# A decoder trunk: whole normalized inputs made beside three biased tiles, later tiles multiplied side by side

## The chip, the cores and the metric

One Trainium2 chip (trn2), one core. The metric is the device time of one execution in microseconds (us); the median of the runs shown is compared. The engines are TensorE (PE; its weight loads are PEld), VectorE (DVE), ScalarE (ACT), GpSimd (POOL) and SyncE (SP, which issues the loads).

## What is computed

```
x = x + 0.5 * gate * swiglu(modulate(x), w_in, w_out)      # FFN 1 (layer 0), FFN 3 (layer 1)
x = x + gate * mixer(modulate(x))                          # retention (layer 0), short_conv (layer 1)
x = x + 0.5 * gate * swiglu(modulate(x), w_in, w_out)      # FFN 2 (layer 0), FFN 4 (layer 1)
out = rmsnorm(x, final_g)

def modulate(x, g, shift, scale): return rmsnorm(x, g) * (1 + scale) + shift
def swiglu(h, w_in, w_out):       gate, up = h @ w_in (halves);  return (silu(gate) * up) @ w_out
def short_conv(h, ...):           b, c, u = h @ w_in (thirds);   return (b * conv_w3(c * u)) @ w_out
```

Two layers, 256 tokens, width 1024, FFN width 2816. Shift, scale and gate come from `silu(c) @ ada_w + ada_b`, a vector times 75 MB of weights.

## The kernel before, in words

Activations lie transposed: eight tiles `x[k]` of 128 features by 256 tokens. All products have float32 accuracy: a weight block w and an input h are each split into a high part `hi`, rounded to float32r, and a low part `lo`, the exact rest, and w h is summed as hi_w hi_h + hi_w lo_h + lo_w hi_h (`product`, line 273). Where the two input halves lie side by side and the PSUM row is wide enough (line 282), the first two are one 512-column matmul whose halves are added later; else there are three matmuls.

Weights stream through five raw buffers. `prepare` (line 250) splits a tile of 2048 columns in two pieces of 1024: ACT casts `hi` (line 243), DVE or, for one piece in six, POOL subtracts `lo` (line 248). There are six `hi` and six `lo` buffers, three tiles' worth; `AHEAD` keeps four tiles in the program's order of loading. Between them `run_side` and `reduce_loaded` run the ada work: one DVE reduction of 128x1024 per half of an ada tile (line 119), paced by `pace`.

An FFN makes 22 projection tiles, each of two sums over eight blocks (`projections`, line 289), then the output products; the convolution makes 12 projection tiles. The RMS norm's factor r (one number per token) isn't known when the projections start, so they run on h = x * scale, and `normalized` (line 302) multiplies the sums by r in one DVE operation. The shift enters through two extra columns (`S1 = S + 2`): line 390 puts the shift's split into columns 256 and 257 of h, a matmul has 258 columns, and the projection's own bias comes out in column 256, to be added by the later activation (`bias=y[:, 0, S:S + 1]`, lines 553 to 556, 725 to 728 and 746 to 748). `modulated` (line 411) issues tile 1 of a sublayer block by block (`by_part`), then the sum of squares over features (line 338), the root on ACT (line 350) and its reciprocal r on DVE (line 356). `retention` works on the same h and is not changed.

The order of the instructions on each engine isn't written by hand but laid out by the Tile scheduler from the program's order and its priorities; an engine runs its own list strictly in that order. PSUM has four pairs of banks (`banks`, line 79); one holds a copy of `cond` from the 11th tile of FFN 1 on (line 567).

Of the kernel before, what the change touches and what calls it, by code (L numbers as in the profile page):

```python
# [14 lines left out]
P = 128  # L15
D = 1024
S = 256
# [11 lines left out]
DEPTH = 2  # L29
PRIO = 300  # L30
LATE = 5
AHEAD = 4
FILL = 8
PARTS = (((0, 2, 0, 0), (5, 8, 1, 1), (2, 5, 0, 0)), ((0, 3, 0, 1), (6, 8, 1, 0), (3, 6, 0, 1)))
# [31 lines left out]
def trunk_kernel(ctx: ExitStack, tc: tile.TileContext, a: dict, out: bass.AP):  # L66
# [4 lines left out]
    wraw_p = ctx.enter_context(tc.tile_pool(name="wraw", bufs=5))  # L71
    whi_p = ctx.enter_context(tc.tile_pool(name="whi", bufs=6))
    wlo_p = ctx.enter_context(tc.tile_pool(name="wlo", bufs=6))
    slot_p = ctx.enter_context(tc.tile_pool(name="slot", bufs=22))
    xhl_p = ctx.enter_context(tc.tile_pool(name="xhl", bufs=1))
    tmp = ctx.enter_context(tc.tile_pool(name="tmp", bufs=2))
    psum = ctx.enter_context(tc.tile_pool(name="psum", bufs=4, space=bass.MemoryType.PSUM))
# [6 lines left out]


    misc = const.tile([P, C_END], F32, name="misc")
    cond = const.tile([P, D], F32, name="cond")
    table = const.tile([P, T_END], F32, name="table")
    ones = const.tile([P, P], F32, name="ones")
    eps = const.tile([P, 1], F32, name="eps")  # L90
# [144 lines left out]
    def split_high(raw, width, w, step=SPLIT):  # L235

        c = w["done"]
        m = min(step, width - c)
        if c % SPLIT == 0:
            hi, lo = whi_p.tile([P, SPLIT], F32R, name="hi"), wlo_p.tile([P, SPLIT], F32R, name="lo")  # L240
            w["parts"].append((hi, lo))
        hi, lo = (part[:, c % SPLIT:c % SPLIT + m] for part in w["parts"][-1])
        nc.scalar.copy(out=hi, in_=raw[:, c:c + m])  # L243
        w["done"] += m
        return lo, raw[:, c:c + m], hi.bitcast(F32)
# [40 lines left out]
                nc.tensor.matmul(out=ps, lhsT=hi, rhs=m[:, 1], start=False, stop=False)  # L286
            nc.tensor.matmul(out=ps[:, :n], lhsT=lo, rhs=m[:, 0], start=False, stop=stop)  # L287

    def projections(h, by_part=False):

        ps, w = banks(), weights()
        n = h[0].shape[-1]
        if by_part:
            for k in range(KB):
                for i in range(2):
                    product(ps[:, i, :n], w, i * KB + k, [h[k]], k == 0, k == KB - 1)
        else:
            for i in range(2):
                product(ps[:, i, :n], w, i * KB, h, True, True)
        return ps  # L300

    def normalized(ps, r, n=S1):

# [101 lines left out]
    def fill(n):  # L405

        ps = banks()[:, 1, :P]
        for _ in range(n):
            nc.tensor.matmul(out=ps, lhsT=ones, rhs=cond[:, :P], start=True, stop=True)

    def modulated():

        h = norm.pop("h")
        state["after"] = norm.pop("made")
        ps = projections(h, True)
        std = rms([norm.pop("acc")], D)  # L420
        with behind():
            load_table(AF.Silu, std)
            return h, inverse(std), std, ps

    def first_modulated():

        l, s = sublayers[0]
        parts = []
        engines = {mybir.EngineType.Activation, mybir.EngineType.DVE, mybir.EngineType.Pool}
        with tc.manual_schedule(engines=engines):  # L430
            for i, pair in enumerate(x_pairs):
                nc.sync.dma_start(out=pair, in_=a["x"][:, 2 * i:2 * i + 2, :])
# [12 lines left out]
            for k in range(KB):  # L445
                ada_reduce(l, s, k, ada.pop(), True)
                if k % 2 == 0:
                    pair = tmp.tile([P, 2, S], F32, name=f"xs{k}", bufs=1)
                xs = pair[:, k % 2, :]
                nc.scalar.activation(out=xs, in_=x[k], func=AF.Copy, scale=scale_t[l][s][:, k:k + 1])  # L450
                raw, width, w = load(2)
                if k + 1 < KB:
                    ada.append(ada_load(l, s, k + 1, 2))
                first = split_high(raw, width, w, 512)
                h = xhl_p.tile([P, 2, HALF], F32R, name=f"h{k}")[:, :, :S]
                parts.append(halves(l, s, k, xs, std, h))
                plain.append((xs, raw))
                split_low(*first, nc.vector)
                for c in range(1, WHOLE // 512):
                    split_low(*split_high(raw, width, w, 512), nc.vector)  # L460
                if k == 1:
                    load_table(AF.Silu, std)
            r = inverse(std)
        state["after"] = [i.ins for i in parts[-1][1:]]
        return [p[0] for p in parts], r
# [72 lines left out]
                    nc.tensor.matmul(out=out, lhsT=lo, rhs=h[k][:, 0], start=False, stop=stop)  # L538
        return [ps.rearrange("p (n s) -> p n s", s=S) for ps in pss]

    def ffn(n, h, r, begun=None):
        act = []

        def activate(ps):
            n = h[0].shape[-1]
            y = normalized(ps, r, n)
            sg = tmp.tile([P, S], F32, name="sg")
            av = tmp.tile([P, S], F32, name="av", bufs=3)
            if n == S:
                nc.scalar.activation(out=sg, in_=y[:, 0, :S], func=AF.Silu)  # L550
                nc.vector.tensor_tensor(out=av, in0=sg, in1=y[:, 1, :S], op=ALU.mult)
            else:
                nc.scalar.activation(out=sg, in_=y[:, 0, :S], func=AF.Silu, bias=y[:, 0, S:S + 1])  # L553
                nc.vector.scalar_tensor_tensor(  # L554
                    out=av, in0=y[:, 1, :S], scalar=y[:, 1, S:S + 1], in1=sg, op0=ALU.add, op1=ALU.mult
                )
            t = in_halves(slot(F32R, "act"))
            split(t, av, nc.gpsimd)
            act.append(t)

        for ps in first_projections(h) if n == 0 else [begun]:
            activate(ps)
        while len(act) < FB:
            activate(projections(h))
            if n == 0 and len(act) == KEEP:
                kept = banks().rearrange("p n c -> p (n c)")
                nc.scalar.copy(out=kept, in_=cond)
                state["cond"] = kept
# [147 lines left out]
        for d in range(2, KB):  # L716
            output(n, d, [(weights(), 0, gated)])

    def short_conv(n, h, r, begun):
        gated = []  # L720

        def taps(d, y, cv):
            u = tmp.tile([P, S], F32, name="u", tag="sg")
            z = tmp.tile([P, S], F32, name="z", tag="av", bufs=3)
            nc.scalar.activation(out=u, in_=y[:, 1, :S], func=AF.Identity, bias=y[:, 1, S:S + 1])
            nc.vector.scalar_tensor_tensor(
                out=z, in0=y[:, 0, :S], scalar=y[:, 0, S:S + 1], in1=u, op0=ALU.add, op1=ALU.mult
            )
            tap = [misc[:, C_CONV + i * KB + d:C_CONV + i * KB + d + 1] for i in range(3)]
            nc.scalar.activation(out=cv, in_=z, func=AF.Copy, scale=tap[2])  # L730
            for i, sh in ((1, 1), (0, 2)):
                nc.vector.scalar_tensor_tensor(
                    out=cv[:, sh:], in0=z[:, :S - sh], scalar=tap[i], in1=cv[:, sh:], op0=ALU.mult, op1=ALU.add
                )

        convs = []
        for d in range(KB):
            if d % 2 == 0:
                pair = slot(F32, "conv")
            convs.append(pair[:, d % 2 * S:(d % 2 + 1) * S])  # L740
            taps(d, normalized(projections(h) if d else begun, r), convs[d])
        for d2 in range(KB // 2):
            y = normalized(projections(h), r)
            for i in range(2):
                yc = y[:, i, :S]
                nc.vector.scalar_tensor_tensor(
                    out=yc, in0=yc, scalar=y[:, i, S:S + 1], in1=convs[2 * d2 + i], op0=ALU.add, op1=ALU.mult
                )
                t = in_halves(slot(F32R, "yg"))
                split(t, yc, nc.gpsimd if d2 < KB // 2 - 1 else nc.vector)  # L750
                gated.append(t)
# [8 lines left out]

    for n, (l, s) in enumerate(sublayers):
        if n == 0:
            ffn(n, *first_modulated())
            continue
        h, r, std, begun = modulated()
        if s != 1:
            ffn(n, h, r, begun)
        elif l % 2 == 0:
            retention(n, h, r, std, begun)
        else:  # L770
            short_conv(n, h, r, begun)
# [87 lines left out]
```

## Time and profile before

| | us |
|---|---|
| runs shown (3) | 1109.13, 1111.17, 1112.13; median 1111.17 |
| profiled execution, its own time | 1109.17 |
| its span | 1107.4 |
| PE busy | 1073.8 |
| DVE, ACT, POOL busy | 850.2, 575.4, 387.7 |
| FFN 2's projections and output stage | 427.9 to 556.5, 556.5 to 618.8 |
| FFN 3's projections and output stage | 618.8 to 747.0, 747.0 to 809.3 |
| convolution's projections | 809.3 to 879.8 |
| FFN 4's projections | 903.3 to 1034.4 |

The profile shows one execution. Busy time counts an engine's instructions; the chain of waits follows the work that ended last back to what released it. A row of instructions gives start, duration, engine, line, operation, output <- inputs. Matmuls are pipelined, so their durations overlap: what a stretch of matmuls costs is read from the start of its first to the start of what follows.

### The profile page before, as it was taken

How to read it: one execution, taken by the hardware profiler on the slowest of the kernel's cores; microseconds unless marked ns; L12 is line 12 of the kernel's file. 1: busy time of each engine (PE TensorE's matmuls, PEld its weight loads, DVE VectorE, ACT ScalarE, POOL GpSimd, SP SyncE). 2: the span in 40 equal slices, each digit the busy share in tenths (PEclk: the TensorE clock that was granted, in tenths of full speed). 3: DMA queues.
4: the chain of work that ended last, by engine and by line, in shares of the span. 5: the costliest groups of instructions: out<-in, count | busy, mean ns of one | idle time of the engine just before them, and what ended most of it. 6: DMA issues, size and time to landing. Idle time of an engine off the chain costs nothing.

```text
span 1107.4 us, 19630 instructions
## 1 busy us (share of the span) xinstructions
PE 1073.8 (97%) x7790; PEld 1019.1 (92%) x7790; DVE 850.2 (77%) x1118; ACT 575.4 (52%) x918; POOL 387.7 (35%) x345
## 2 busy tenths in 40 slices
PE   8999999997899999999999999999999989999996
PEld 7999988996779989999988999998899989999985
DVE  5999777999559888887768778776798786666354
ACT  4464454732357666455455655445565475454452
POOL 0034356344024631333355232335511532223352
PEclk9999999998999999999999999999999999999998
DMA  9977789855465777786669867667886535454441
GB/s 348 354 272 277 295 283 316 308 205 190 190 228 191 265 249 278 289 312 247 244 225 321 326 251 301 253 229 252 313 300 253 175 138 207 167 191 132 157 131 39
DMA packets 44574, 268.52 MB, mean 242 GB/s; under 512 B 4801, under 2 KB 6977, under 8 KB 19906
## 3 DMA queue, kind: packets, MB, share of 16 engines
q1 hardware_dynamic: 43138, 266.56, 66.4%
q8 instruction: 61, 1.00, 0.4%
q10 hardware_dynamic: 1344, 0.71, 0.2%
q14 instruction: 31, 0.25, 0.1%
HBM read 266.20 MB, written 1.05 MB: 241 GB/s over the span
## 4 chain that ended last, share of the span: by engine, by line
PE 58%; DVE 2%; issue 0%; ACT 0%; DVEq 0%; ACTq 0%
PE ps L287 19%; PE ps L286 14%; PE ps L285 14%; PE ps L283 10%; DVE lo L248 1%; PE ps L338 0%; DVE rsum L475 0%; DVE h L392 0%; DVE raw L781 0%; DVE r L777 0%; DVE x L478 0%; ACT hi L243 0%; DVEq L854 0%; DVE x L480 0%; ACT std L350 0%
## 5 line engine op out<-in xcount | busy, mean ns | idle before, releaser
L248 DVE TENSOR_TENSOR lo<-raw,hi 128x1024 fp32r<-128x1024 f32 (+1 forms) x300 | 363.1, 1218 | 174.8 <-ACT hi L243 144.6
L285 PE MATMUL ps<-h,hi 128*128 128x258 f32 (+1 forms) x1728 | 490.2, 284 | 3.6 <-DVE sum L610 2.5
L286 PE MATMUL ps<-h,hi 128*128 128x258 f32 (+1 forms) x1728 | 489.9, 283 | 1.6 <-DVE h L392 1.5
L287 PE MATMUL ps<-h,lo 128*128 128x258 f32 (+1 forms) x1728 | 490.3, 284 | 0.0
L243 ACT CAST hi<-raw 128x1024 fp32r<-128x1024 f32 (+2 forms) x408 | 377.3, 937 | 205.8 <-PE ps L286 104.5
L285 PEld LDWEIGHTS ps<-h,hi 128*128 128x128 f32 x1728 | 329.4, 191 | 4.5 <-issue 3.2
L286 PEld LDWEIGHTS ps<-h,hi 128*128 128x128 f32 x1728 | 329.0, 190 | 2.6 <-DVE h L392 1.3
L287 PEld LDWEIGHTS ps<-h,lo 128*128 128x128 f32 x1728 | 329.0, 190 | 0.0
L248 POOL TENSOR_TENSOR lo<-raw,hi 128x384 fp32r<-128x384 f32 (+1 forms) x108 | 203.2, 1882 | 311.4 <-ACT hi L243 302.0
L283 PE MATMUL ps<-act,hi 128*128 128x512 f32 x616 | 216.0, 395 | 0.6 <-DVE rsum L475 0.6
L287 PE MATMUL ps<-act,lo 128*128 128x256 f32 x704 | 197.4, 280 | 0.0
L312 POOL TENSOR_TENSOR act<-av,act 128x256 fp32r<-128x256 f32 x88 | 84.4, 961 | 250.6 <-ACT act L311 241.5
L119 DVE CUSTOM_DVE_ANT_0 raw<-raw,ps,misc 128x1024 f32<-128x1024 f32 x124 | 154.4, 1273 | 0.0
L283 PEld LDWEIGHTS ps<-act,hi 128*128 128x128 f32 x616 | 115.4, 187 | 28.1 <-DVE rsum L475 1.7
L287 PEld LDWEIGHTS ps<-act,lo 128*128 128x128 f32 x704 | 133.1, 189 | 0.3 <-DVE lo L248 0.3
L311 ACT CAST act<-av 128x256 fp32r<-128x256 f32 x88 | 35.5, 405 | 100.8 <-DVE av L554 78.6
L305 DVE TENSOR_TENSOR sum<-ps,r 128x516 f32<-128x516 f32 (+1 forms) x108 | 73.9, 688 | 16.1 <-PE ps L287 15.8
L554 DVE SCALAR_TENSOR_TENSOR av<-sum,sg 128x256 f32<-128x256 f32 x66 | 51.8, 784 | 17.6 <-ACT sg L553 17.6
L553 ACT ACTIVATE sg<-sum 128x256 f32<-128x256 f32 x66 | 33.5, 508 | 25.7 <-DVE sum L305 25.5
L321 ACT ACTIVATE sq<-x 128x256 f32<-128x256 f32 x48 | 19.8, 416 | 49.5 <-DVE x L478 42.3
L328 POOL TENSOR_TENSOR acc<-acc,sq 128x256 f32<-128x256 f32 x32 | 27.1, 846 | 36.9 <-ACT sq L321 34.4
L283 PE MATMUL ps<-og,hi 128*128 128x512 f32 x112 | 38.9, 391 | 0.0
(126 smaller groups left out, 1079.2 us busy)
## 6 DMA issues: line engine op xcount, KB each, us to landing
raw<-in_ffn_in SPq DMA_DIRECT2D x80, 1024.0 KB, 4.9
raw<-in_ada_w SPq DMA_DIRECT2D x64, 1024.0 KB, 5.7
raw<-in_ffn_out SPq DMA_DIRECT2D x64, 704.0 KB, 5.0
raw<-in_ada_w SPq DMA_DIRECT2D x16, 512.0 KB, 6.1
raw<-in_ffn_in SPq DMA_DIRECT2D x16, 512.0 KB, 7.0
raw<-in_ret_qk SPq DMA_DIRECT2D x8, 1024.0 KB, 6.4
raw<-in_ret_v SPq DMA_DIRECT2D x8, 1024.0 KB, 4.9
raw<-in_ret_g SPq DMA_DIRECT2D x8, 1024.0 KB, 4.8
```

Of the source, the lines that this page charges most:

```text
L119: ins = nc.vector.tensor_tensor_reduce(out=w, in0=w, in1=state["cond"], scale=1.0, scalar=misc[:, C_ADAB + 72 * l + col:C_ADAB + 72 * l + ...
L243: nc.scalar.copy(out=hi, in_=raw[:, c:c + m])
L248: eng.tensor_tensor(out=lo, in0=raw, in1=hi, op=ALU.subtract)
L283: nc.tensor.matmul(out=ps, lhsT=hi, rhs=m.rearrange("p n s -> p (n s)"), start=start, stop=False)
L285: nc.tensor.matmul(out=ps, lhsT=hi, rhs=m[:, 0], start=start, stop=False)
L286: nc.tensor.matmul(out=ps, lhsT=hi, rhs=m[:, 1], start=False, stop=False)
L287: nc.tensor.matmul(out=ps[:, :n], lhsT=lo, rhs=m[:, 0], start=False, stop=stop)
L305: nc.vector.tensor_tensor(out=y[:, :, :n], in0=ps[:, :, :n], in1=r[:, :n].unsqueeze(1).to_broadcast([P, 2, n]), op=ALU.mult)
L311: hi = nc.scalar.copy(out=dst[:, 0], in_=src)
L312: lo = eng.tensor_tensor(out=dst[:, 1], in0=src, in1=dst[:, 0].bitcast(F32), op=ALU.subtract)
L553: nc.scalar.activation(out=sg, in_=y[:, 0, :S], func=AF.Silu, bias=y[:, 0, S:S + 1])
L554: nc.vector.scalar_tensor_tensor(out=av, in0=y[:, 1, :S], scalar=y[:, 1, S:S + 1], in1=sg, op0=ALU.add, op1=ALU.mult)
```

## The change

In FFNs 2 to 4 and the convolution the first three projection tiles stay as they were (`BIASED = 3`). Beside them a new function `whole` makes the complete normalized input, x * r * scale + shift, split in halves that lie side by side in eight slots, and the remaining tiles multiply these: 512 columns for the high weights, 256 for the low, no bias columns, no r behind them. The two halves of each sum are added by an ACT copy of the second and a DVE addition of the first. The fourth tile is issued block by block. The slot pool grows from 22 to 30, `cond` moves from a constant to one of the six `hi` buffers (and to PSUM later, as before), and four pairs `xs` of FFN 1 move into slots.

```diff
+BIASED = 3
...
-    slot_p = ctx.enter_context(tc.tile_pool(name="slot", bufs=22))
+    slot_p = ctx.enter_context(tc.tile_pool(name="slot", bufs=30))
...
-    cond = const.tile([P, D], F32, name="cond")
+    cond = whi_p.tile([P, D], F32, name="cond", tag="hi")
...
-    def projections(h, by_part=False):
+    def projections(h, by_part=False, side=False):
...
-        n = h[0].shape[-1]
+        n = h[0].shape[-1] * (2 if side else 1)
...
+    def projected(src):
+
+        src["used"] += 1
+        if src["used"] <= BIASED:
+            y = normalized(src.pop("begun") if src["used"] == 1 else projections(src["h"]), src["r"])
+            return y, [y[:, i, S:S1] for i in range(2)]
+        ps = projections(src["whole"], src["used"] == BIASED + 1, True)
+        y = tmp.tile([P, 2, HALF], F32, name="sum")
+        nc.scalar.copy(out=y[:, :, :S], in_=ps[:, :, S:])
+        nc.vector.tensor_tensor(out=y[:, :, :S], in0=ps[:, :, :S], in1=y[:, :, :S], op=ALU.add)
+        return y, None
...
+    def whole(n, r):
+
+        l, s = sublayers[n]
+        parts = []
+        for k in range(KB):
+            xr = tmp.tile([P, S], F32, name="xr", tag="sq", bufs=3)
+            (nc.gpsimd if k % 2 else nc.vector).tensor_tensor(out=xr, in0=x[k], in1=r[:, :S], op=ALU.mult)
+            nc.scalar.activation(
+                out=xr, in_=xr, func=AF.Identity, scale=scale_t[l][s][:, k:k + 1],
+                bias=mod[l][:, 24 * s + k:24 * s + k + 1],
+            )
+            h = in_halves(slot(F32R, "whole"))
+            split(h, xr, nc.vector)
+            parts.append(h)
+        return parts
...
-                    pair = tmp.tile([P, 2, S], F32, name=f"xs{k}", bufs=1)
+                    pair = in_halves(slot(F32, "xs"))
...
-    def ffn(n, h, r, begun=None):
+    def ffn(n, src=None, h=None, r=None):
...
-        for ps in first_projections(h) if n == 0 else [begun]:
-            activate(ps)
+        if n == 0:
+            for ps in first_projections(h):
+                activate(normalized(ps, r, S), None)
+        else:
+            src["whole"] = whole(n, src["r"])
         while len(act) < FB:
-            activate(projections(h))
+            if n:
+                activate(*projected(src))
+            else:
+                activate(normalized(projections(h), r, S), None)
...
-    def short_conv(n, h, r, begun):
+    def short_conv(n, src):
         gated = []
+        src["whole"] = whole(n, src["r"])
...
-            taps(d, normalized(projections(h) if d else begun, r), convs[d])
+            taps(*projected(src), convs[d])
         for d2 in range(KB // 2):
-            y = normalized(projections(h), r)
+            y, _ = projected(src)
```

In `activate` and `taps` a tile without bias uses plain products where a biased one adds the bias in the same operation, and `taps` then needs no `u`.

How the order moves, at the start of FFN 3. First DVE's list, from the reciprocal on. Before (`lo` is a weight subtraction, `sum` the evacuation of a projection tile, `av` the product of gate and up):

```order
L356 RECIPROCAL r<-std 128x256
L248 TENSOR_TENSOR lo<-raw,hi 128x1024
L305 TENSOR_TENSOR sum<-ps,r 128x2x258
L248 TENSOR_TENSOR lo<-raw,hi 128x1024
L554 SCALAR_TENSOR_TENSOR av<-sum,sg 128x256
L305 TENSOR_TENSOR sum<-ps,r 128x2x258
L248 TENSOR_TENSOR lo<-raw,hi 128x1024
```

And with the change (`xr` is x times r, `whole` the low half of a part; of the eight `xr` four are here, the others on POOL):

```order
L375 RECIPROCAL r<-std 128x256
L249 TENSOR_TENSOR lo<-raw,hi 128x1024
L436 TENSOR_TENSOR xr<-x_91,r 128x256
L436 TENSOR_TENSOR xr<-x_92,r 128x256
L324 TENSOR_TENSOR sum<-ps,r 128x2x258
L249 TENSOR_TENSOR lo<-raw,hi 128x1024
L331 TENSOR_TENSOR whole<-xr,whole 128x256 x3
L436 TENSOR_TENSOR xr<-x_93,r 128x256
L586 SCALAR_TENSOR_TENSOR av<-sum,sg 128x256
L324 TENSOR_TENSOR sum<-ps,r 128x2x258
L249 TENSOR_TENSOR lo<-raw,hi 128x1024
L331 TENSOR_TENSOR whole<-xr,whole 128x256 x2
```

The parts' steps stand between evacuations and weight subtractions, which keep their sequence; after the rows shown come one more `xr`, an `av`, a `whole`, the evacuation of tile 3, a `lo` and the last two `whole`.

Then ACT's list at the same place with the change, from the second of two weight casts behind the root on (`sg` is the silu of a biased tile):

```order
L244 CAST hi<-raw 128x1024 x2
L437 ACTIVATE xr<-xr,mod_96,sc_100 128x256 x3
L330 CAST whole<-xr 128x256 x3
L319 ACTIVATE sg<-sum 128x256
L244 CAST hi<-raw 128x1024
L437 ACTIVATE xr<-xr,mod_96,sc_100 128x256 x2
L330 CAST whole<-xr 128x256 x2
L437 ACTIVATE xr<-xr,mod_96,sc_100 128x256
```

Before, the casts and the silu stood there alone; the first activation of a part now stands behind a cast that waits for a `hi` buffer.

## Rows read from the trace of the kernel before

**Rows 1.** The page: busy time, share of the span, instructions of each engine.

```profile
PE 1073.8 (97%) x7790; PEld 1019.1 (92%) x7790; DVE 850.2 (77%) x1118; ACT 575.4 (52%) x918; POOL 387.7 (35%) x345
```

**Rows 2.** The page: chain that ended last, share of the span by engine, by line.

```profile
PE 58%; DVE 2%; issue 0%; ACT 0%; DVEq 0%; ACTq 0%
PE ps L287 19%; PE ps L286 14%; PE ps L285 14%; PE ps L283 10%; DVE lo L248 1%; PE ps L338 0%; DVE rsum L475 0%; DVE h L392 0%; DVE raw L781 0%; DVE r L777 0%; DVE x L478 0%; ACT hi L243 0%; DVEq L854 0%; DVE x L480 0%; ACT std L350 0%
```

**Rows 3.** PE in projection stretches: start:end length, busy (instructions), granted clock, DMA share, GB/s.

```profile
434.80:556.51 121.71, 121.71 (x1010) 1.00 0.73 268
618.79:624.55 5.76, 5.76 (x51) 1.00 1.03 393
624.79:747.05 122.26, 122.26 (x1010) 1.00 0.71 260
815.36:879.77 64.41, 64.41 (x530) 1.00 0.65 231
912.16:1034.43 122.27, 122.27 (x1011) 1.00 0.50 171
```

**Rows 4.** The same in output stages of FFN 2 and the convolution.

```profile
579.59:610.33 30.74, 30.74 (x176) 1.00 0.91 322
880.12:898.84 18.72, 18.72 (x110) 1.00 0.41 154
```

**Rows 5.** Groups by form: count, busy us, mean ns; idle us before, its releasers.

```profile
L248 DVE TENSOR_TENSOR lo<-raw,hi 128x1024 fp32r<-128x1024 f32 x276 | 348.0, 1264 | 174.8 <-ACT hi L243 144.6 <-PE ps L287 29.4
...
L119 DVE CUSTOM_DVE_ANT_0 raw<-raw,ps,misc 128x1024 f32<-128x1024 f32 x124 | 154.4, 1273 | 0.0
...
L305 DVE TENSOR_TENSOR sum<-ps,r 128x512 f32<-128x512 f32 x22 | 14.6, 681 | 0.2
...
L672 ACT COPY o<-ps 128x512 f32<-128x512 f32 x8 | 4.5, 584 | 0.0
...
L725 ACT ACTIVATE u<-sum 128x256 f32<-128x256 f32 x8 | 4.1, 509 | 6.1 <-DVE sum L305 6.1
...
L312 DVE TENSOR_TENSOR hv<-xs,hv 128x256 fp32r<-128x256 f32 x8 | 3.3, 413 | 0.1
L311 ACT CAST hv<-xs 128x256 fp32r<-128x256 f32 x8 | 3.2, 406 | 30.2 <-DVE xs L402 30.2
```

**Rows 6.** Waits, first 145 us: engine line <- waited for: us, times, longest.

```profile
ACT act L311 <- DVE av L551: 20.9, 12, 2.8
```

**Rows 7.** Instructions of POOL from 447 to 638: start, us, what.

```profile
447.83 2.40 POOL L248 TENSOR_TENSOR lo<-raw,hi 128x1024 fp32r<-128x1024 f32 x1 [1.91 <-ACT hi L243]
...
635.20 1.47 POOL L312 TENSOR_TENSOR act<-av,act 128x256 fp32r<-128x256 f32 x1 [6.09 <-ACT act L311]
637.48 0.74 POOL L312 TENSOR_TENSOR act<-av,act 128x256 fp32r<-128x256 f32 x1 [0.80 <-ACT act L311]
```

**Rows 8.** Instructions of DVE in the same stretch.

```profile
447.92 3.39 DVE L248 TENSOR_TENSOR lo<-raw,hi 128x1024 fp32r<-128x1024 f32 x1
451.24 0.47 DVE L554 SCALAR_TENSOR_TENSOR av<-sum,sg 128x256 f32<-128x256 f32 x1
...
636.00 0.96 DVE L554 SCALAR_TENSOR_TENSOR av<-sum,sg 128x256 f32<-128x256 f32 x1
```

**Rows 9.** DVE at the start of FFN 3.

```profile
628.88 1.75 DVE L356 RECIPROCAL r<-std 128x256 f32<-128x256 f32 x1
630.55 1.16 DVE L248 TENSOR_TENSOR lo<-raw,hi 128x1024 fp32r<-128x1024 f32 x1
```

**Rows 10.** ACT at the start of FFN 3.

```profile
630.86 1.06 ACT L243 CAST hi<-raw 128x1024 fp32r<-128x1024 f32 x1 [1.79 <-PE ps L286]
```

**Rows 11.** DVE at the starts of FFN 2, the convolution and FFN 4.

```profile
436.50 1.75 DVE L356 RECIPROCAL r<-std 128x256 f32<-128x256 f32 x1
...
817.72 1.74 DVE L356 RECIPROCAL r<-std 128x256 f32<-128x256 f32 x1
...
913.06 1.75 DVE L356 RECIPROCAL r<-std 128x256 f32<-128x256 f32 x1
```

More of the change, by code (lines that the diff above doesn't have):

```diff
@@ L239, in split_high @@
         if c % SPLIT == 0:
-            hi, lo = whi_p.tile([P, SPLIT], F32R, name="hi"), wlo_p.tile([P, SPLIT], F32R, name="lo")
+            hi, lo = whi_p.tile([P, SPLIT], F32R, name="hi", tag="hi"), wlo_p.tile([P, SPLIT], F32R, name="lo")
             w["parts"].append((hi, lo))
@@ L300, in projections, with silu @@
         return ps
+    def projected(src):
[8 more added lines that the diff above has]
+        return y, None
+    def silu(y, i, bias, out):
+        if bias is None:
+            nc.scalar.activation(out=out, in_=y[:, i, :S], func=AF.Silu)
+        else:
+            nc.scalar.activation(out=out, in_=y[:, i, :S], func=AF.Silu, bias=bias[i][:, :1])
     def normalized(ps, r, n=S1):
@@ L539, in first_projections, with activate @@
         return [ps.rearrange("p (n s) -> p n s", s=S) for ps in pss]
-    def ffn(n, h, r, begun=None):
+    def ffn(n, src=None, h=None, r=None):
         act = []
-        def activate(ps):
-            n = h[0].shape[-1]
-            y = normalized(ps, r, n)
+        def activate(y, bias):
             sg = tmp.tile([P, S], F32, name="sg")
             av = tmp.tile([P, S], F32, name="av", bufs=3)
-            if n == S:
-                nc.scalar.activation(out=sg, in_=y[:, 0, :S], func=AF.Silu)
+            silu(y, 0, bias, sg)
+            if bias is None:
                 nc.vector.tensor_tensor(out=av, in0=sg, in1=y[:, 1, :S], op=ALU.mult)
             else:
-                nc.scalar.activation(out=sg, in_=y[:, 0, :S], func=AF.Silu, bias=y[:, 0, S:S + 1])
                 nc.vector.scalar_tensor_tensor(
-                    out=av, in0=y[:, 1, :S], scalar=y[:, 1, S:S + 1], in1=sg, op0=ALU.add, op1=ALU.mult
+                    out=av, in0=y[:, 1, :S], scalar=bias[1][:, :1], in1=sg, op0=ALU.add, op1=ALU.mult
                 )
@@ L559, in activate @@
             act.append(t)
-        for ps in first_projections(h) if n == 0 else [begun]:
-            activate(ps)
+        if n == 0:
[3 more added lines that the diff above has]
+            src["whole"] = whole(n, src["r"])
         while len(act) < FB:
-            activate(projections(h))
+            if n:
+                activate(*projected(src))
+            else:
+                activate(normalized(projections(h), r, S), None)
             if n == 0 and len(act) == KEEP:
@@ L717, in retention, with taps @@
             output(n, d, [(weights(), 0, gated)])
-    def short_conv(n, h, r, begun):
+    def short_conv(n, src):
         gated = []
-        def taps(d, y, cv):
-            u = tmp.tile([P, S], F32, name="u", tag="sg")
+        src["whole"] = whole(n, src["r"])
+        def taps(y, bias, cv):
             z = tmp.tile([P, S], F32, name="z", tag="av", bufs=3)
[L725 to L728, printed above, removed]
+            if bias is None:
+                nc.vector.tensor_tensor(out=z, in0=y[:, 0, :S], in1=y[:, 1, :S], op=ALU.mult)
+            else:
+                u = tmp.tile([P, S], F32, name="u", tag="sg")
+                nc.scalar.activation(out=u, in_=y[:, 1, :S], func=AF.Identity, bias=bias[1][:, :1])
+                nc.vector.scalar_tensor_tensor(
+                    out=z, in0=y[:, 0, :S], scalar=bias[0][:, :1], in1=u, op0=ALU.add, op1=ALU.mult
+                )
             tap = [misc[:, C_CONV + i * KB + d:C_CONV + i * KB + d + 1] for i in range(3)]
@@ L740, in short_conv @@
             convs.append(pair[:, d % 2 * S:(d % 2 + 1) * S])
-            taps(d, normalized(projections(h) if d else begun, r), convs[d])
+            taps(*projected(src), convs[d])
         for d2 in range(KB // 2):
-            y = normalized(projections(h), r)
+            y, _ = projected(src)
             for i in range(2):
                 yc = y[:, i, :S]
-                nc.vector.scalar_tensor_tensor(
-                    out=yc, in0=yc, scalar=y[:, i, S:S + 1], in1=convs[2 * d2 + i], op0=ALU.add, op1=ALU.mult
-                )
+                nc.vector.tensor_tensor(out=yc, in0=yc, in1=convs[2 * d2 + i], op=ALU.mult)
                 t = in_halves(slot(F32R, "yg"))
@@ L762, in trunk_kernel @@
         if n == 0:
-            ffn(n, *first_modulated())
+            ffn(n, None, *first_modulated())
             continue
         h, r, std, begun = modulated()
+        src = {"h": h, "r": r, "begun": begun, "used": 0}
         if s != 1:
-            ffn(n, h, r, begun)
+            ffn(n, src)
         elif l % 2 == 0:
@@ L770, in trunk_kernel @@
         else:
-            short_conv(n, h, r, begun)
+            short_conv(n, src)
     std = rms([norm.pop("last")], D, norm.pop("bank")[:, 0, :S])
```

## The prediction

> **What bounds the kernel now.** I read the engines' busy times first: TensorE (PE) is busy 1073.8 of 1107.4 us, the vector engine (DVE) 850.2, the scalar engine (ACT) 575.4, GpSimd (POOL) 387.7 [rows 1]. The chain that ended last agrees: 58% of the span stands on PE and 2% on DVE, and the four matmul lines of `product` carry nearly all of it [rows 2]. So the stages touched here are paid in TensorE time, and another engine counts only where TensorE waits for it.
>
> Next I cut the projection stages out of the trace, for the pace of one weight block (128x128, 16 to a tile). Tiles 2 to 22 of FFN 2 take 121.71 us, of FFN 3 122.26 and of FFN 4 122.27; tiles 2 to 12 of the convolution 64.41 us [rows 3]. (A window's count holds two or three matmuls that began before it: 1010 is 21 x 48 and two more.) With 336 and 176 blocks that is 0.3622, 0.3639, 0.3639 and 0.3660 us a block of three 258-column matmuls. The output stage of FFN 2 already multiplies both halves side by side: 30.74 us for 87 blocks, 0.3533 us a block of one 512- and one 256-column matmul [rows 4]. The granted clock is 1.00 in all of these, the 2.4 GHz level, with no idle time, so this is a difference of pace and not of waiting.
>
> **The gain.** 19 tiles of each FFN and 9 of the convolution change over: 3 x 19 x 16 + 9 x 16 = 1056 blocks, two matmuls each instead of three. At the output stage's pace: FFN 2 304 x 0.0089 = 2.7 us, FFN 3 and FFN 4 304 x 0.0106 = 3.2 each, the convolution 144 x 0.0126 = 1.8. **Sum: 10.9 us less.** The lower bound is what tile 1 of FFN 3 shows: taken block by block its 16 blocks cost 5.76 us, 0.3600 each [rows 3], and 1056 x 0.0067 = 7.0 us. The upper bound is a block of the convolution's output, where four sums take turns: 18.72 us for 54 blocks, 0.3467 [rows 4], 1056 x 0.018 = 19 us. I take the output stage of the FFN, since the new tiles run as it does, one sum at a time.
>
> A rule speaks against that size. The Trainium skill, "TensorE: Matmul & The Clock Gate", section "Wait — 56ns, not 53.3ns?", has warm matmuls follow each other after N columns at 2.4 GHz plus some 2.5 ns; worked out (an estimate) that is 330 ns for the old block and 325 for the new, and the gain would be 5.3 us instead of 10.9. The rows decide: both blocks are slower than that by unequal amounts.
>
> **What is added beside TensorE.** The nearest prices [rows 5]: an ACT activation of 128x256 0.51 us, a cast 0.41, a DVE subtraction 0.41, a PSUM copy by ACT of 128x512 0.58, a DVE operation on 128x512 out of PSUM 0.68. Back to back each costs some 0.08 less: the subtraction at 630.55 begins before 628.88 + 1.75 [rows 9]. A later tile swaps `normalized` (0.68) for an ACT copy and a DVE addition of that size: DVE stays level, ACT gets 66 x 0.58 = 38 us more. The u activations that go, and additions of the bias that become plain products of one price, are nothing. ACT rises from 52% to under 60%. A PSUM pair is let go one ACT step later; one of four pairs holds `cond`, three turn over, and the pair of tile n is wanted two tiles (11 us) after its end: nothing. The casts of the shift columns move forward in time, off TensorE's path: nothing.
>
> The buffers: `cond` now sits in one of six `hi` buffers until tile 11 of FFN 1. Where ACT idles in the first 145 us it is for DVE, 20.9 us before the act casts alone, and no cast there waits for TensorE [rows 6]; with 5 buffers a cast may wait for the half tile before, which is done. Nothing; bound 0 to 2 us. SP's loads keep their order, and so do TensorE, DVE and POOL through FFN 1 and the retention.
>
> **What is added ahead of TensorE: `whole`.** At each start 8 products x*r (4 on DVE, 4 on POOL), 8 activations, 8 casts and 8 subtractions must be done while tiles 2 and 3 run, since tile 4 goes block by block through the eight parts. Only three `xr` buffers turn over, so POOL's second product waits for the first subtraction. And DVE and POOL hinder each other: a POOL product that found a DVE subtraction running took 1.47 us instead of 0.74 [rows 7], the DVE product after that subtraction 0.96 instead of 0.47, and a DVE subtraction met by POOL's own (2.40 us) took 3.39 instead of 1.2 [rows 7, 8]. So each POOL product costs DVE up to 0.72 us.
>
> I walk FFN 3's start through the new order. r is there at 630.6 and DVE first has a subtraction until 631.6 [rows 9]; POOL's product then goes first, to 632.35; DVE's two products, tile 1's evacuation and a weight subtraction last until 634.7. ACT's weight cast waits for TensorE and ends at 631.9 [rows 10]; three activations and three casts then end at 634.7. Parts 0 to 2 are done, with POOL's second product among them, at 636.4. A DVE product, POOL's third, av, tile 2's evacuation and a weight subtraction follow to 639.3, so part 3 is ready at 639.7, 4 at 640.1. TensorE starts tile 4 at 624.79 + 2 x 5.82 = 636.4, uses 0.71 us a part, and wants part 3 at 638.55. Part 5 comes at 641.7; an evacuation and a weight subtraction come ahead of parts 6 and 7, 643.8 and 644.1. Tile 4 ends at 645.3 instead of 642.1: **3.2 us late.** The same walk without the hindrance of POOL ends 1.0 us late: the two bounds of a start.
>
> FFN 2 and the convolution have r at 438.2 and 819.5 [rows 11], 8.1 and 7.6 us before tile 4 (FFN 3 has 5.8), but the gap is filled by ada reductions on DVE, 1.27 us a half [rows 5]: the walks give 2.8 and 2.8. FFN 4 has r at 914.8, 9.0 us before tile 4, and no ada work: 0. Sum 8.8 us with every hindrance, about 3 without any. POOL was given every tie in the first walk, and in the rows the loser's tail overlaps the winner; I take the middle, **5.9 us**. What is late next is nothing: weight parts are made two tiles ahead, and the walk puts them back by under 4 us of those 11.
>
> **Sum.** -10.9 + 5.9 = -5.0 us. The profiled execution took 1109.17 us (1107.4 of span and 1.8 around it), 2.0 below the median of 1111.17; against the median the forecast is **1106.1 us**. A measurement of this kernel tells about 0.3% (3.3 us) from no change.
>
> **Rivals.**
> - *The parts are ready in time.* For it: DVE idles 174.8 us before weight subtractions as a whole [rows 5]. Against: at the three starts DVE has none to spare. Waits of 3 us or less: -8 us, 1103.2. Chance 0.20.
> - *Every tie is lost.* Waits of 8.8 us: -2.1, 1109.0, no change to be told. Chance 0.13.
> - *Only columns and instructions are paid.* If the old block's pace above 0.3600 comes from traffic that stays, the gain is 7.0 and the sum -1.1: 1110.1. For it: tile 1 does run at that pace. Against: it alternates two sums, which the later tiles don't. Chance 0.10. The page's rule above is of this kind; by its figures the time would be 1111.8.
> - *Slower: POOL's weight subtraction takes the port ahead of parts 3 to 7.* In the queues of FFN 2 and the convolution such a one (2.4 us, as in [rows 8]) stands near them. At three starts that makes 8.8 + 7.2 = 16 us of waiting against 10.9 gained: +5.1, 1116.3. It decides from 14.3 us of waiting in all, 4.8 a start; in the walks POOL's subtraction falls beside the ada reductions, which it doesn't hinder. Chance 0.11.
> - That the change doesn't do what it says is excluded by the order: 1056 matmuls of 512 and 1056 of 256 on `whole` take the place of 3168 of 258.
>
> My forecast keeps 0.46. Faster by over 0.3% (below 1107.8) comes from the first rival, 0.20, and most of the forecast's own spread (starts of 1 to 3 us), 0.38: 0.58. Within 0.3%: the rest of it and the second and third rivals, 0.31. Slower: 0.11. The range 1102.0 to 1112.0 reaches from waits of about 2 us in all to waits of 11.8; 2 in 10 lie outside.
>
> **What would show it.** Tiles 5 to 22 at 0.353 us a block (5.65 us a tile; FFN 4's 18 tiles in 101.8 us); PE idle at L284 behind DVE `whole`, 1 to 3 us at each of three starts, none in FFN 4; FFN 1 and the retention as before. A pace near 0.360, or starts over 4.8 us, would make the forecast wrong, and so would a new wait of PE for a PSUM pair or weights within tiles 5 to 22.

## The result, and the profile after

The changed kernel takes **1102.12 us** (median of 4 runs, 1099.74 to 1105.26) against 1111.24 of the kernel before (4 runs): a ratio of 0.9923, 95% interval 0.9909 to 0.9937. That is 0.77% faster, so the sign was right. The forecast was 1106.1, and the time lies just inside the lower end of its range. The profiled execution is the slowest of the four, 1105.26 us with a span of 1103.4, 3.9 us below the profiled one of before.

Busy times and the chain of waits of the page after, to be held against [rows 1] and [rows 2]:

```profile
PE 1064.7 (96%) x6734; PEld 959.4 (87%) x6734; DVE 861.4 (78%) x1166; ACT 621.3 (56%) x1043; POOL 401.4 (36%) x361
...
PE 53%; DVE 6%; issue 1%; ACT 0%; DVEq 0%; ACTq 0%
```

TensorE has 1056 matmuls fewer and 9.1 us less to do, but the span fell by only 4.0: part of the gain became waiting, and DVE's share of the chain went from 2% to 6%. ACT rose by 46 us. DVE's additions wait 23.6 us in all for ACT's copies, but ACT keeps 0% of the chain that ended last.

PE in the four stretches that run on `whole` (FFN 2, FFN 3, the convolution, FFN 4; columns as there), which answer to [rows 3]:

```profile
446.35:555.60 109.25, 107.94 (x611) 1.00 0.73 271
635.18:745.12 109.94, 108.32 (x611) 1.00 0.72 261
824.70:879.58 54.88, 52.64 (x290) 0.97 0.61 215
924.09:1029.47 105.38, 105.38 (x610) 1.00 0.51 178
```

FFN 2, FFN 3 and FFN 4 do the same 304 blocks there, and FFN 4 is 3.9 and 4.6 us faster than the others. Part of that is waiting (busy is below length in the first three). The rest is pace: the last 160 blocks of the FFNs, and 96 of the convolution, in the same order and without any idle time:

```profile
498.71:555.24 56.53, 56.53 (x323) 1.00 0.69 259
688.23:744.77 56.54, 56.54 (x323) 1.00 0.72 263
845.31:879.23 33.92, 33.92 (x194) 1.00 0.56 191
973.66:1029.13 55.47, 55.47 (x323) 1.00 0.46 159
```

Divided by the blocks: 0.3533, 0.3534, 0.3533 and **0.3467** us. The granted clock is 1.00 in all four. So the same pair of matmuls has two paces 0.0066 us apart, and it holds one of them for a whole stretch that has no wait in it.

Next come the waits of PE that the change made, summed over the whole program, and then the convolution's start cut into windows (before the wait, the wait, after it, later):

```profile
PE ps L284 <- DVE whole L331: 5.2, 6, 2.2
```

```profile
828.17:828.90 0.73, 0.73 (x6) 1.00 0.95 404
828.90:831.31 2.41, 0.17 (x3) 1.00 1.01 425
831.31:834.57 3.26, 3.26 (x10) 0.52 1.03 407
834.95:838.00 3.05, 3.05 (x19) 1.00 0.09 35
```

These are 5.2 us in six waits: 1.3 in FFN 2, 1.6 in FFN 3, 2.2 in the convolution, none in FFN 4. Behind the convolution's wait the granted clock is 0.52, near the 1.2 GHz level, for five blocks, which take 0.65 us each instead of 0.35: 1.5 us more that no idle time shows. What DVE did in that wait:

```profile
824.87 1.27 DVE L120 CUSTOM_DVE_ANT_0 raw<-raw,ps,misc 128x1024 f32<-128x1024 f32 x1
...
827.08 0.97 DVE L331 TENSOR_TENSOR whole<-xr,whole 128x256 fp32r<-128x256 f32 x1
827.97 0.68 DVE L324 TENSOR_TENSOR sum<-ps,r 128x516 f32<-128x516 f32 x1
828.58 2.34 DVE L249 TENSOR_TENSOR lo<-raw,hi 128x1024 fp32r<-128x1024 f32 x2
830.84 0.75 DVE L331 TENSOR_TENSOR whole<-xr,whole 128x256 fp32r<-128x256 f32 x2
```

An evacuation and two weight subtractions, 3.0 us, stand ahead of parts 6 and 7, and two ada reductions stood further up. No wait of TensorE for weights shows here; it waits for what is queued behind them.

By stages, from the first projection to the first output matmul, before and after: FFN 2 128.60 and 127.95 us, FFN 3 128.26 and 127.81, the convolution 70.42 and **72.75**, FFN 4 131.08 and **126.70**. In this execution nearly the whole gain is FFN 4's, and the convolution lost 2.3 us.

### The profile page after: what moved, and what is told of

Read it like the earlier page. It is cut to its first block, busy times and chain, and to the rows that moved or that the text cites. A ratio compares the mean times of both kernels' runs of the same rounds, so it can differ in the third digit from the quotient of the medians.

```text
span 1103.4 us, 17725 instructions
## 1 busy us (share of the span) xinstructions
PE 1064.7 (96%) x6734; PEld 959.4 (87%) x6734; DVE 861.4 (78%) x1166; ACT 621.3 (56%) x1043; POOL 401.4 (36%) x361
## 4 chain that ended last, share of the span: by engine, by line
PE 53%; DVE 6%; issue 1%; ACT 0%; DVEq 0%; ACTq 0%
PE ps L284 32%; PE ps L288 18%; DVE lo L249 2%; PE ps L287 2%; PE ps L286 1%; DVE raw L120 1%; DVE whole L331 1%; DVE xr L436 0%; DVE r L375 0%; DVE h L411 0%; DVE sum L324 0%; DVE av L586 0%; DVE rsum L510 0%; DVE raw L822 0%; PE ps L357 0%
## 5 line engine op out<-in xcount | busy, mean ns | idle before, releaser
L284 PE MATMUL ps<-whole,hi 128*128 128x512 f32 x1056 | 373.7, 398 | 5.2 <-DVE whole L331 5.2
L288 PE MATMUL ps<-whole,lo 128*128 128x256 f32 x1056 | 296.8, 281 | 0.0
L284 PEld LDWEIGHTS ps<-whole,hi 128*128 128x128 f32 x1056 | 198.8, 188 | 54.7 <-DVE whole L331 7.3
L288 PEld LDWEIGHTS ps<-whole,lo 128*128 128x128 f32 x1056 | 200.3, 190 | 0.0
L286 PE MATMUL ps<-h,hi 128*128 128x258 f32 (+1 forms) x672 | 191.7, 285 | 3.1 <-DVE sum L648 2.5
L287 PE MATMUL ps<-h,hi 128*128 128x258 f32 (+1 forms) x672 | 190.9, 284 | 2.0 <-DVE h L411 1.8
L288 PE MATMUL ps<-h,lo 128*128 128x258 f32 (+1 forms) x672 | 190.1, 283 | 0.0
L286 PEld LDWEIGHTS ps<-h,hi 128*128 128x128 f32 x672 | 128.1, 191 | 3.8 <-issue 2.7
L287 PEld LDWEIGHTS ps<-h,hi 128*128 128x128 f32 x672 | 128.2, 191 | 3.2 <-DVE h L411 2.8
L288 PEld LDWEIGHTS ps<-h,lo 128*128 128x128 f32 x672 | 128.0, 190 | 0.0
L312 DVE TENSOR_TENSOR sum<-ps,sum 128x512 f32<-128x512 f32 x66 | 45.3, 686 | 23.6 <-ACT sum L311 23.6
L584 DVE TENSOR_TENSOR av<-sg,sum 128x256 f32<-128x256 f32 x79 | 51.3, 653 | 13.7 <-ACT sg L317 13.7
```

Source lines behind the costliest of these rows:

```text
L284: nc.tensor.matmul(out=ps, lhsT=hi, rhs=m.rearrange("p n s -> p (n s)"), start=start, stop=False)
L286: nc.tensor.matmul(out=ps, lhsT=hi, rhs=m[:, 0], start=start, stop=False)
L312: nc.vector.tensor_tensor(out=y[:, :, :S], in0=ps[:, :, :S], in1=y[:, :, :S], op=ALU.add)
```

## The experiments

The view behind them was that the time is made of three things: the two paces, which each stage takes anew in each execution; the start waits; and the half clock behind one of them. Each run had its own theories A and B, which its expectation states.

**The changed kernel again**, no edit.

> The changed kernel once more, nothing edited. Theory A (a block of one 512- and one 256-column matmul has two paces, 0.3467 and 0.3533 us, and a stage takes one or the other anew in each execution): in this execution at least one of the stages in which such blocks run stands at the other pace than in the first trace (there FFN 2, FFN 3 and the convolution 0.3533, FFN 4 0.3467), each FFN that flips moves by 304 x 0.0066 = 2.0 us, and the runs spread over several us. Theory B (the pace belongs to the place in the program): the same stages at the same pace, and the runs' spread comes from waits.

It took 1101.58 us (1098.58 to 1106.60, 6 runs), a ratio of 0.9929 (0.9907 to 0.9951) against 1109.52. The same four stretches at the end of each stage:

```profile
498.37:554.91 56.54, 56.54 (x322) 1.00 0.70 258
687.08:742.54 55.46, 55.46 (x322) 1.00 0.73 266
843.69:877.61 33.92, 33.92 (x195) 1.00 0.55 190
971.90:1027.37 55.47, 55.47 (x323) 1.00 0.45 159
```

FFN 3 has gone from 0.3534 to 0.3466 with the same program, and the profiled time is 1.9 us lower than the first (1103.41). That is theory A. The waits came back alike: 5.2 us in six, and behind the convolution's wait of 2.2 us again 3.20 us (from 830.91 on) at a granted clock of 0.50. Over the seven traces of this study that run these stages side by side at 256 columns without an added matmul, FFN 2 stood at 0.3467 three times, FFN 3 four times, FFN 4 seven times, and the convolution three times out of six at its end. The count has an order in it, read over the traces and not tried by a run of its own: nine of these FFN stretches began without a wait (FFN 4 in all seven traces, FFN 3 in the two where four tiles are biased there), and all nine stood at 0.3467. The other eighteen stretches had a wait at or near their start (FFN 2 seven, FFN 3 five, the convolution six), and behind it eight stood at 0.3467.

**The kernel before again**, no edit, one execution.

> The kernel before once more, nothing edited: what its blocks of three 258-column matmuls take in another execution. Theory A (they too have a pace that is taken anew in each stage of each execution): FFN 2, FFN 3, the convolution and FFN 4 stand at other values than 0.3622, 0.3639, 0.3660 and 0.3639 us, within some 0.360 to 0.366, and FFN 2 to 4's output stages swap 0.3467 and 0.3533. Theory B (only the pair of 512 and 256 has two paces): the four values come back within 0.0003.

It took 1110.59 us. Tiles 2 to 22 or 2 to 12 of the four stages:

```profile
434.87:556.58 121.71, 121.71 (x1011) 1.00 0.72 268
624.88:747.70 122.82, 122.82 (x1011) 1.00 0.71 260
816.01:880.44 64.43, 64.43 (x531) 1.00 0.64 231
912.81:1035.08 122.27, 122.27 (x1011) 1.00 0.50 171
```

Three of the four are back within 0.02 us of [rows 3]; FFN 3 has gone from 122.26 to 122.82, 0.0017 us a block. So the old block moves too, by a quarter of what the pair does. Neither theory was quite right. The longer stretches of the output stages of FFN 2 and FFN 3 stood at 0.3533 in both traces of this kernel, that of FFN 4 at 0.3467 in the first and 0.3533 in the second.

**One more matmul ahead of each half tile**, one execution. The added matmul's sum is overwritten by the next. There are 124 of them, since the fourth tile, issued block by block, gets none; the expectation's 132 counts it in.

```
 for k, m in enumerate(moving):
     hi, lo = columns(w, (at + k) * P)
+    if ps.shape[-1] == 2 * n and k == 0 and len(moving) == KB and first and last:
+        nc.tensor.matmul(out=ps[:, :P], lhsT=hi, rhs=m[:, 0, :P], start=True, stop=True)
```

> The changed kernel with one more matmul of 128 columns ahead of each half tile of eight blocks on whole (its sum is overwritten by the next matmul): 132 of them. Theory A (the pace, 0.3467 or 0.3533 us a block, is a matter of where the stream of matmuls stands, and an odd matmul in it sets it anew): within one FFN some half tiles run at 0.3467 and some at 0.3533, or all at one value in every stage; the time is up by 132 x about 0.07 = 9 us less what the pace gives. Theory B (the pace belongs to the stage of an execution, whatever the stream): one value within each FFN and still both among the stages.

It took 1118.63 us. Six blocks of four half tiles in a row in FFN 2 (from the second block's start to the eighth's):

```profile
480.06:482.18 2.12, 2.12 (x14) 1.00 0.37 77
482.99:485.11 2.12, 2.12 (x14) 1.00 1.01 410
485.92:488.00 2.08, 2.08 (x14) 1.00 0.56 236
488.82:490.94 2.12, 2.12 (x14) 1.00 0.97 386
```

0.3533, 0.3533, 0.3467, 0.3533, and so on: two slow, one fast, through FFN 2 and in the same turn of three in the other stages. The DMA share goes up and down beside it without bearing on it. So the pace isn't a matter of the stage or of the traffic: an odd matmul in the stream moves it on, as theory A had it. The time is 17 us over the changed kernel's 1101.58, more than the 9 expected: by its start times the added matmul costs 0.06 us itself and 0.05 more in the block behind it (0.40 instead of 0.35), which makes 14 us.

**Three matmuls of 256 columns on the whole input.** Without the second sum, the copy and the addition fall away, and what follows reads PSUM itself. In the convolution a copy of u by ACT and a tile for the last products come in (not shown).

```
-        ps = projections(src["whole"], src["used"] == BIASED + 1, True)
-        y = tmp.tile([P, 2, HALF], F32, name="sum")
-        nc.scalar.copy(out=y[:, :, :S], in_=ps[:, :, S:])
-        nc.vector.tensor_tensor(out=y[:, :, :S], in0=ps[:, :, :S], in1=y[:, :, :S], op=ALU.add)
-        return y, None
+        return projections(src["whole"], src["used"] == BIASED + 1), None
```

> The whole input stays, but later tiles multiply it in three matmuls of 256 columns instead of 512 and 256; the evacuation then needs no copy and no addition. Theory A (a matmul fewer a block is what gains): three matmuls of 256 take 0.360 us a block, as in the alternating sums of the outputs, and 1056 x 0.010 = 10 us are lost, near 1112. Theory B (the two shift columns, 258 instead of 256, are what cost): 0.350 us a block as in FFN 1's tiles, which is the mean of the two paces of the pair, so the time stays near 1102 with TensorE running 1056 matmuls more.

It took 1113.32 us (11 runs), a ratio of 1.0035 (1.0023 to 1.0047): slower than before. 96 blocks of FFN 2:

```profile
480.19:514.75 34.56, 34.56 (x290) 1.00 0.74 276
```

That is 0.3600 us a block, and FFN 3, FFN 4 and the convolution end at the same pace. The waits are as they were (4.9 us). Theory A. Dropping the two shift columns alone takes 0.0022 to 0.0060 us off the old block of [rows 3]; the 1056 blocks gain 3.9 us by that, less than the start waits cost. The rest of the gain is in the two matmuls side by side, 0.0067 to 0.0133 us a block more.

**Four biased tiles everywhere.**

```
-BIASED = 3
+BIASED = 4
```

> BIASED 4 in place of 3: the parts have one tile (5.8 us) more before TensorE wants them. Theory A (the starts cost TensorE 1.9 us in FFN 2, 2.1 in FFN 3 and 4.0 in the convolution, where a wait of 2.4 us is followed by 3.3 us at half clock): the idle time behind whole goes from 5.2 us to under 0.5, the half clock in the convolution goes with it, and 4 x 16 blocks at the old pace cost 64 x 0.010 = 0.6 us: 7 us faster than the changed kernel, near 1095. Theory B (the scheduler sets the parts one tile later as well, since they are wanted later): waits as before, 0.6 us slower, near 1103.

It took 1097.60 us (1096.19 to 1098.44), a ratio of 0.9887 (0.9867 to 0.9906): 4.0 us below the changed kernel on the same chip, not 7. The waits behind `whole` are gone, and in the convolution the half clock with them: its projections take 69.5 us instead of 72.75, and with four biased tiles the change gains there too (70.42 before). FFN 3, without a wait, runs at 0.3467. But FFN 2 has a wait of another kind. PE at its tile 5, the clock from there on, and DVE ahead of it:

```profile
451.66 0.47 PE L284 MATMUL ps<-whole,hi 128*128 128x512 f32 x1 [1.75 <-DVE sum L324]
```

```profile
449.90:451.66 1.76, 0.01 (x2) 1.00 0.75 265
451.66:456.50 4.84, 4.84 (x19) 0.65 0.74 266
```

```profile
448.77 2.13 DVE L331 TENSOR_TENSOR whole<-xr,whole 128x256 fp32r<-128x256 f32 x1
450.83 0.68 DVE L324 TENSOR_TENSOR sum<-ps,r 128x516 f32<-128x516 f32 x1
```

Tile 5 wants the PSUM pair of tile 2, and DVE evacuates that one only behind a part whose subtraction took 2.13 us instead of 0.41, beside POOL's weight subtraction (448.22, 2.39 us). The wait and the clock behind it (4.84 us for 9.5 blocks, 1.5 more than at 0.3533 each) cost 3.2 us together, more than the 1.8 that FFN 2's start had cost, so FFN 2 lost by it (129.75 us instead of 127.95).

**The convolution as before**, the FFNs as changed: `whole` isn't made there, all 12 tiles take the biased way, and the last products add the bias again.

```
 def short_conv(n, src):
     gated = []
-    src["whole"] = whole(n, src["r"])
...
-        if src["used"] <= BIASED:
+        if src["used"] <= (BIASED if "whole" in src else KB + KB // 2):
```

> The convolution alone as in the kernel before (all 12 tiles with shift columns, no whole input); the FFNs as changed. Theory A (in the convolution the start, 4.0 us, costs more than 144 blocks at the faster pace bring, 144 x 0.0126 = 1.8): its projections go from 72.75 us back to 70.4, 2 us faster than the changed kernel, near 1100. Theory B (the convolution gains like the FFNs and its longer projections are an accident of that execution): 1.8 us slower, near 1104.

It took 1099.82 us (1097.63 to 1101.81), 1.8 below the changed kernel; the runs of the two overlap. The trace is plainer than the time: the convolution's projections take 70.1 us, and with the change they take 72.75 and 72.77 in its two traces. Theory A, for three biased tiles.

**Eight buffers for the products x*r**, and then, these kept, **all eight products on DVE**.

```
+        pairs = [in_halves(slot(F32, "xr")) for _ in range(KB // 2)]
         for k in range(KB):
-            xr = tmp.tile([P, S], F32, name="xr", tag="sq", bufs=3)
+            xr = pairs[k // 2][:, k % 2, :]
```

```
-            (nc.gpsimd if k % 2 else nc.vector).tensor_tensor(out=xr, in0=x[k], in1=r[:, :S], op=ALU.mult)
+            nc.vector.tensor_tensor(out=xr, in0=x[k], in1=r[:, :S], op=ALU.mult)
```

> The changed kernel (three biased tiles everywhere) with eight xr buffers (two to a slot) in place of three that turn over. Theory A (the parts are late because DVE's list is full: each part's subtraction stands behind evacuations, weight subtractions and ada reductions): TensorE's idle time behind whole stays near 5.2 us and the half clock in the convolution stays; no difference in time. Theory B (the buffers hold the parts up: POOL's product waits 2.8 us for a subtraction to free one): idle time under 2 us, no half clock, 4 to 5 us faster, near 1097.

> As the run before, and all eight products x*r of a start on DVE, none on POOL. Theory A (POOL's products hinder DVE, and cost it about as much as doing them itself would, 0.33 us each): waits of TensorE within 1.5 us of the run before. Theory B (the products on POOL are the dear part, by the 0.5 us that DVE operations grow beside them): waits 2 us or more below the run before. If DVE's list is full, as theory A of that run has it, they rise instead, by up to 3 x 1.3 us.

They took 1106.85 us (10 runs, ratio 0.9969, 0.9957 to 0.9980) and 1101.29 us (4 runs, 0.9918, 0.9902 to 0.9935). PE's waits behind `whole`, of the first and of the second:

```profile
PE ps L284 <- DVE whole L331: 8.3, 6, 2.0
```

```profile
PE ps L284 <- DVE whole L331: 3.7, 5, 1.4
```

More buffers made it worse, which neither theory had: with them free the scheduler laid the parts out two at a time, further apart in DVE's list, so the last two stand later. Nor is it only that DVE's list is full, as theory A had it: in FFN 3 DVE stood idle for 1.75 us ahead of the third pair, behind a weight subtraction that waited for ACT's cast:

```profile
643.48 1.23 DVE L249 TENSOR_TENSOR lo<-raw,hi 128x1024 fp32r<-128x1024 f32 x1 [1.75 <-ACT hi L244]
```

With the products on DVE the waits fall by 4.6 us, as theory B had it. The lists were laid out anew here too, so how much of the 4.6 is POOL's hindrance isn't shown. It is seen in single rows: at FFN 3's start the first two products and the first `av` took DVE 1.31 and 0.97 us in the changed kernel, and 0.75 and 0.48 here. Against the changed kernel no gain in time is shown (1101.29 and 1101.58): 1.5 us less of waiting is within the spread of these runs.

**Three biased tiles in FFN 2 and FFN 4, four in FFN 3 and the convolution.**

```
-        if src["used"] <= BIASED:
+        if src["used"] <= src["biased"]:
...
-        src = {"h": h, "r": r, "begun": begun, "used": 0}
+        src = {"h": h, "r": r, "begun": begun, "used": 0, "biased": BIASED + (n in (3, 4))}
```

> Three biased tiles in FFN 2 and FFN 4, four in FFN 3 and the convolution. Four everywhere took TensorE's waits behind whole away, but in FFN 2 a wait of 1.75 us for the evacuation of tile 2 came in their place, and FFN 4 had no wait to lose. Theory A: FFN 2's start as in the changed kernel (1.9 us), FFN 3's and the convolution's without a wait and without half clock: 0.3 us faster than four everywhere, the same within what can be told, near 1097.3, and some 5 us faster than the changed kernel. Theory B (what four gained came from paces that were lucky in its runs): no better than the changed kernel, near 1101.

It took **1095.56 us** (1094.99 to 1096.88), a ratio of 0.9868 (0.9851 to 0.9884): the fastest of the study. Its four stretches on `whole`:

```profile
446.09:553.46 107.37, 105.99 (x611) 1.00 0.75 276
639.37:739.21 99.84, 99.84 (x578) 1.00 0.76 277
825.21:870.40 45.19, 44.67 (x259) 1.00 0.64 232
914.67:1020.06 105.39, 105.39 (x611) 1.00 0.51 178
```

FFN 2 waits 1.4 us, FFN 3 and FFN 4 not at all, the convolution 0.5 without a fall of the clock. This trace has the fast pace in all four stages. FFN 3 and FFN 4, without a wait, have it in every such trace; FFN 2 and the convolution might have had the other, so the profile flatters the kernel somewhat. The four runs lie within 1.9 us. That is theory A, which put this kernel level with four biased tiles everywhere: their two ratios can't be told apart.

## Why the prediction was right, and where it was off

- **What bounds, and the sign.** Right. TensorE's time fell by the pace of the blocks, and DVE counted only at the starts.
- **The gain.** This term was mis-sized. The prediction read 0.3533 from FFN 2's output stage as the pace of one sum at a time, and put 0.3467 in the convolution's output down to four sums that take turns. Both are paces of the same pair: FFN 4 ran one sum at a time at 0.3467 in every trace. The trace of before shows it too, in the first 37 blocks of the same output stage of FFN 2, one sum at a time, 0.3467 each:

```profile
556.51:569.34 12.83, 12.83 (x77) 1.00 0.74 238
```

  Over the eighteen stretches with a wait the mean is 0.3504. With that for FFN 2, FFN 3 and the convolution and 0.3467 for FFN 4, the gain against the old block of [rows 3] is 304 x 0.0118 + 304 x 0.0135 + 144 x 0.0156 + 304 x 0.0172 = 15.2 us instead of 10.9. It lies between the forecast's bounds of 7.0 and 19 (by the rows the upper one is 304 x 0.0155 + 608 x 0.0172 + 144 x 0.0193 = 18).
- **The rule weighed there.** The Trainium skill, "TensorE: Matmul & The Clock Gate", section "Wait — 56ns, not 53.3ns?", gives by its figures (estimates) 330 and 325 ns a block and a gain of 5.3 us. The traces disagree with it on both blocks, by 0.032 to 0.036 us for the old block and by 0.022 or 0.028 for the new. Taking the rows was right.
- **The start waits.** The term was 5.9, the second one mis-sized. What a start cost is the length of its stretch on `whole` less the blocks at the pace that the stretch then held: 109.25 - 304 x 0.3533 = 1.8 us in FFN 2, 2.5 in FFN 3, 54.88 - 144 x 0.3533 = 4.0 in the convolution, 8.4 together (8.6 in the second trace). The middle between the walks had 1.9, 2.1 and 1.9: near for the FFNs, half of what came in the convolution. That FFN 4 has none was right. Of the 8.4, 5.2 are idle time and 1.5 the half clock, and the fall of the clock behind a wait was missing from the walk. Some 1.0 more (an estimate) comes from how idle time is counted: a 256-column matmul is drawn 0.28 us long while the next starts 0.12 us after it, and a wait counts only from the drawn end, 0.16 us short, six times. The last 0.7 us are not assigned.
- **Sum.** In the two traces the two terms nearly make up the difference. In the first, with the slow pace in FFN 2, FFN 3 and the convolution, 12.9 us were gained and 8.4 lost, -4.5, and the profiled executions differ by -3.9; in the second, with FFN 3 fast, it is -14.9 + 8.6 = -6.3 against -5.8. With the mean paces it is -15.2 + 8.4 = -6.8, while the medians differ by -9.1, -7.0 to -10.1 by the interval of the ratio. Both profiled executions of the changed kernel were slower than the median of their runs; which paces the others had isn't on record, and some 2 us of the gain stay open. The two mis-sized terms, 4.3 us too little gain and 2.5 too little waiting, partly cancel, so that the forecast came within 4.0 us is in part luck.
- **What was costed at nothing.** ACT's 46 us, the later release of PSUM pairs and `cond`'s place showed no wait of TensorE in the four stages, and FFN 2 starts at 427.65 us where it started at 427.91. The PSUM pairs are no safe nothing, though: with four biased tiles FFN 2 waited for one.
- **The rivals.** "The parts are ready in time" is nearest in its number, 1103.2, but not by its mechanism: the starts cost 8.4 us, not 3. "Only columns and instructions are paid" put the old block's pace above 0.3600 down to traffic that stays; it falls with the run of three 256-column matmuls, which took 0.3600 with the same weights streaming. "POOL's weight subtraction takes the port" didn't come in the changed kernel; in the one with four biased tiles it did at one place, where it cost a subtraction of DVE 1.7 us. Another operation of POOL's did come, at FFN 3's start of the changed kernel: beside its subtractions for `act` the last two parts took DVE 1.82 us instead of 0.75, and TensorE waited 0.7 us for them:

```profile
640.97 2.19 POOL L331 TENSOR_TENSOR act<-av,act 128x256 fp32r<-128x256 f32 x2 [0.18 <-ACT act L330]
641.63 1.82 DVE L331 TENSOR_TENSOR whole<-xr,whole 128x256 fp32r<-128x256 f32 x2
```

- **What would show it.** FFN 4's 18 tiles were forecast at 101.8 us; at 0.3467 they are 99.8. PE idles behind DVE `whole` at three starts and not at the fourth, as said.

Shown by runs: the two paces of the pair and that an odd matmul moves the stream from one to the other, the gain of two matmuls side by side over three on the same input, the convolution's loss with three biased tiles, and that one more biased tile takes the waits behind `whole` away. Only argued: the cost of the half clock as a part of its own, since no run took it away without the wait, and POOL's share in the waits.

## What to carry to other kernels

Before a pace is read off one stage of one trace, look for the same form of instruction in every other stage: where it has two values, the next kernel may get either, and the price of a block is a mean of them. Here a stretch that began without a wait always got the faster one. Where work is put ahead of an engine to be ready in time, count in the queue of the engine that makes it what stands ahead of the last piece, and ask whether one more round of the old way costs less than the wait (here 16 blocks x 0.010 us against the 2 to 4 us of a start). And a wait of TensorE can cost more than its length: read the granted clock of the stretch behind it.

## What the runs showed of the hardware that wasn't expected

- A block of a 512- and a 256-column matmul takes 0.3467 or 0.3533 us at a granted clock of 1.00. Most of the difference lies in the step from the start of the 512 to that of the 256: by the mean of some 280 and 300 steps it is 0.236 us in FFN 3 and 0.230 in FFN 4 of the first trace, while the step from the 256 to the next 512 is 0.117 in both. One odd matmul every eight blocks makes the pace go slow, slow, fast in turn. What in the chip has that period stays open.
- The pace can change at a wait. The convolution with four biased tiles came to `whole` without one, and its first 31 blocks stood at 0.3468 us; behind a wait of 0.5 us, the granted clock staying at 1.00, the rest stood at 0.3534:

```profile
826.29:837.04 10.75, 10.75 (x64) 1.00 0.72 274
838.48:872.05 33.57, 33.57 (x193) 1.00 0.65 225
```

  In the run with four tiles in FFN 3 and the convolution alone, the same place kept 0.3467 behind its wait. So a start wait puts the pace of all that follows at risk: 304 blocks x 0.0066 us are 2.0 us for an FFN. Why a stretch without a wait was fast in all nine cases stays open.
- Three matmuls of 256 columns took 0.3600 us a block on `whole`, in the run made for it, but 48 such blocks of FFN 1 in the changed kernel took 16.80 us, 0.3500 each, with the clock at 1.00 as well:

```profile
121.15:137.95 16.80, 16.80 (x146) 1.00 0.57 203
```

  So three matmuls don't always cost more than two. The inputs lie differently in SBUF (in the program, side by side on `whole` and with room for the shift columns between them in FFN 1); whether that is the reason wasn't tried.
- Waits of 2.2 us (convolution) and 1.75 us (FFN 2, four biased tiles) were followed by 3.3 us at 0.52 and 4.8 at 0.65 of the clock; one of 2.0 us in FFN 3 with eight buffers was followed by 4.9 us at 1.00. So the length of the one wait doesn't decide it alone; what else bears on it was not tried.
